# Token sums of the down projection: split where they are made, kept in DRAM in two parts, reloaded as operands

## The chip, the cores and the metric

The kernel runs on one core of one Trainium2 chip. The metric is the device time of one execution in microseconds (us). A core has a matrix engine (TensorE, PE in the profile, with PEld for its weight loads), a vector engine (VectorE, DVE), a scalar engine (ScalarE, ACT), a general engine (GpSimd, POOL) and a sync engine (SyncE, SP) whose queue here issues most of the transfers. Each engine works through its own instructions in order and waits at semaphores for the others. Transfers run on 16 DMA engines that all queues share.

## The reference, cut to what matters

The program is one decoder block on 256 tokens (plus 16 meta tokens) of width 2048: input projections, an RWKV-7 branch and a forgetting-attention branch, a gated merge, and a SwiGLU feed-forward part. The change concerns the last part:

```python
gate, up = jnp.split(_rms(h, n2) @ w_gu, 2, axis=-1)     # [256, 2048] @ [2048, 2 * 5632]
return h + (jax.nn.silu(gate) * up) @ w_dn               # [256, 5632] @ [5632, 2048]
```

Everything is float32. The kernel gets the precision on the matrix engine by splitting each operand in a high part (rounded to the engine's float32r) and a low part (the rest), and adding up high times high, low times high and high times low: three matrix instructions ("matmuls") for each product of blocks.

## The kernel before, in words

**Gate and up.** The hidden activations, transposed, split and normalised, lie in the tile `hts`: 16 slices (one per 128 rows of the contraction), each with a high and a low half of 272 columns, so 2176 bytes per partition and slice. For each of 11 blocks of 512 columns the kernel runs a gate job group and an up job group, each over 8 weight tiles of 512 KB (`raw`, four buffers, loaded by SP's queue). `wload` splits each into `wh` (ScalarE, line 335) and `wl` (VectorE, line 336), four buffers each. Jobs are written so that a tile is loaded and split one job ahead of its matmuls; a list scheduler then sets the final order on ScalarE, VectorE, GpSimd and SP in this part of the program, so that splits run up to three tiles ahead. After a group, `post_up` computes silu(gate) times up for four blocks of 128 columns (`ub`), and splits them into `ach` and `acl`, the operands of the down projection.

**Down.** The contraction of 5632 is cut into 22 pairs of 2 x 128 rows, the output of 2048 columns into two column halves (`cg` 0 and 1) of 1024. Pairs 10 to 21 (`SLOW`, "plain pairs") are done directly: two jobs of four products, so 8 products, 24 matmuls, in the PSUM tiles `dn`. Pairs 0 to 9 (`FAST`, "quads", since each has four jobs) use a Strassen-Winograd scheme: 7 products, 21 matmuls, with sums and differences of weight blocks (`tt`, made by VectorE on the way from the loaded tile `q`, lines 1516, 1523, 1524) and four sums of token blocks (`sx`, lines 1400 and 1401), of which three are operands of their own (`sst`) and the fourth overwrites a block of `ach` and `acl` that is not otherwise used for that pair. Four of the products go to PSUM tiles `dnp`, added at the end of a column half by `sums_of_products`. `ORDER` sets which pair follows which: 2 plain pairs first in column half 0, 1 in column half 1, and then quads and plain pairs in turn.

**The path of the token sums.** `sums_of_tokens` makes the four sums of a quad while the up group ends, and GpSimd's queue stores them in DRAM as float32 (`ss`, 256 KB each). The memory in which they are used later is still that of `hts`, so they cannot stay. Reloading is done two quads at a time by `sums_of` (line 1392) into one tile `sl`; a stream `split_of_sums`, woken about every 9 us of planned matmul time (`PAIRS`), splits it with ScalarE and VectorE (lines 510 and 511) into `sst` and into `ach` and `acl`, and then issues the next reload. The first reload is issued during gate and up; the second needs `sl` free, so it follows the first split, which needs the memory of `hts`, so the end of the last up group.

Of the kernel before, what the change touches and what calls it, by code (L numbers as in the profile page):

```python
# [9 lines left out]
F32 = mybir.dt.float32  # L10
F32R = mybir.dt.float32r
I32 = mybir.dt.int32
AF = mybir.ActivationFunctionType
ALU = mybir.AluOpType
# [4 lines left out]
P = 128  # L19
# [47 lines left out]

FAST = list(range(10))
SLOW = list(range(10, 22))
ORDER = [SLOW[:n] + [i for pair in zip(FAST, SLOW[n:]) for i in pair] + SLOW[n + len(FAST):] for n in (2, 1)]  # L70
PAIRS = 9000

HOP = 3050
SPREAD = 12000
# [2 lines left out]
GAP = 250  # L77
# [37 lines left out]
def hybrid_block(ctx, tc, A, out, dbg=None):  # L115
    nc = tc.nc
# [12 lines left out]
    dp = ctx.enter_context(tc.tile_pool(name="dp", bufs=1, space=DRAM))  # L129

    def main_ps(name):
        return psm.tile([P, 512], F32, tag="main", name=name)
# [176 lines left out]
        nc.tensor.matmul(pz, zw, zw, start=True, stop=True)  # L309


    behind = [None, None]

    def wload(parts, n, between=None, lay=None):

        raw = wp.tile([P, 1024], F32, tag="raw", name="raw", bufs=RAWB)
        wh = wp.tile([P, WCOLS], F32R, tag="wh", name="wh", bufs=WB)
        wl = wp.tile([P, WCOLS], F32R, tag="wl", name="wl", bufs=WB)  # L320
        if lay is not None:


            (_, _, shape, ((_, src),)), = parts
            odd, *first = lay
            nc.sync.dma_start(raw.rearrange("p (k c) -> p k c", c=shape[1]), src)
            if odd is None:
                rr = raw.rearrange("p (r c) -> p r c", c=T)
                th, tl = (t.rearrange("p (r c) -> p r c", c=L)[:, :, s:s + T] for t, s in zip((wh, wl), first))
            else:  # L330
                rr = raw.rearrange("p (j q c) -> p q j c", q=2, c=shape[1])
                th, tl = ((t if odd else t[:, s:s + 1024]).rearrange("p (q e) -> p q e", q=2)
                          [:, :, odd and s:(odd and s) + 512].rearrange("p q (j c) -> p q j c", c=shape[1])
                          for t, s in zip((wh, wl), first))
            behind[0] = nc.scalar.activation(th, rr, AF.Copy)  # L335
            behind[1] = nc.vector.tensor_tensor(tl, rr, th.bitcast(F32), op=ALU.subtract)  # L336
            return [(th, tl)]
        res = []
        for prow, c0, shape, srcs in parts:
            size = 1  # L340
            for d in shape:
                size *= d
            names = " ".join(f"d{i}" for i in range(len(shape)))
            kw = {f"d{i}": d for i, d in enumerate(shape)}

            def v(t):
                return t[:prow, c0:c0 + size].rearrange(f"p ({names}) -> p {names}", **kw)

            for sel, src in srcs:
                nc.sync.dma_start(v(raw)[sel], src)  # L350
            if between is not None:
                between(len(res))
            cs_ = slice(c0, c0 + size)
            nc.scalar.activation(wh[:prow, cs_], raw[:prow, cs_], AF.Copy)
            nc.vector.tensor_tensor(wl[:prow, cs_], raw[:prow, cs_], wh[:prow, cs_].bitcast(F32), op=ALU.subtract)
            res.append((v(wh), v(wl)))
        return res
# [3 lines left out]
    def kblock(ap):  # L361
        return ap.rearrange("(k p) c -> p k c", p=P)
# [13 lines left out]
    def spawn(gen, delay):  # L376
        streams.append([clock[0] + delay, gen, None])
# [44 lines left out]
    def finish_job():  # L422
        if pending:
            pending.pop()()

    def run(jobs):
        for load, mul in jobs:
            w = load()
            finish_job()
            pending.append(lambda w=w, mul=mul: mul(w))  # L430
# [78 lines left out]
    def split(hi, lo_, src):  # L509
        nc.scalar.activation(hi, src, AF.Copy)  # L510
        nc.vector.tensor_tensor(lo_, src, hi.bitcast(F32), op=ALU.subtract)  # L511
# [169 lines left out]
    def rwkv_jobs(g):  # L681
# [19 lines left out]
        def load():  # L701
            cs_ = slice(c0, c0 + 256)
            return wload([(96, 0, [2, 256], [((ALL, 0), A["rwkv_w2"][0][:, cs_]), ((ALL, 1), A["rwkv_a2"][0][:, cs_])]),
                          (P, 512, [2, 256], [((ALL,), kblock(A["rwkv_g2"][0][:, cs_]))])], 1024)
# [596 lines left out]
    hp = hp_pool.__enter__()  # L1301
    hh = hp.tile([P, 2, D], F32, tag="hh", name="hh")

    ht_pool = tc.tile_pool(name="ht", bufs=1, reuse_waits="tile")
    ht = ht_pool.__enter__()
    hts = ht.tile([P, KT, 2, L], F32R, tag="hts", name="hts")
    ss2 = hp.tile([P, 2, 4], F32, tag="ss2", name="ss2")
    rs2 = hp.tile([P, 2], F32, tag="rs2", name="rs2")
# [74 lines left out]
    NF = DFF // P  # L1383
# [2 lines left out]
    wgu = A["w_gate_up"][0]  # L1386
    ssd = {}

    def sums_of(at):
        sl = hp.tile([P, 2, 4, P], F32, tag="sl", name=f"sl{at}", bufs=1)  # L1390
        for x_ in range(2):
            nc.gpsimd.dma_start(sl[:, x_], ssd[FAST[at + x_]])
        return sl

    def sums_of_tokens(i, u0, u1):

        (a11, a21), (a12, a22) = ((u[:, :P], u[:, P:]) for u in (u0, u1))
        sx = ht.tile([P, 512], F32, tag="jk", name=f"sx{i}", bufs=2).rearrange("p (n c) -> p n c", n=4)
        for n, x_, y_, op in ((0, a21, a22, ALU.add), (1, sx[:, 0], a11, ALU.subtract), (2, a11, a21, ALU.subtract),
                              (3, a12, sx[:, 1], ALU.subtract)):  # L1400
            nc.vector.tensor_tensor(sx[:, n], x_, y_, op=op)
        d = ssd[i] = dp.tile([P, 4, P], F32, tag=f"ss{i}", name=f"ss{i}")
        nc.gpsimd.dma_start(d, sx)

    for j in range(DFF // 512):
        gs = [ht.tile([P, T], F32, tag="ga", name=f"ga{j}{m}", bufs=8) for m in range(4)]
# [26 lines left out]

    wdn = A["w_down"][0]
    fast = FAST
    sums0 = sums_of(0)
    slow = [i for i in range(NF // 2) if i not in fast]
    acp_h, acp_l = (t.rearrange("p (i k) (t c) -> p i k t c", k=2, t=2) for t in (ach, acl))
    finish_job()
    ht_pool.__exit__(None, None, None)  # L1440
    dn_pool = tc.tile_pool(name="dnp", bufs=1, reuse_waits="tile")
    dn = dn_pool.__enter__()
    sst = dn.tile([P, len(fast), 3, 2, P], F32R, tag="sst", name="sst")

    def split_of_sums(sl):

        for at in range(0, len(fast), 2):
            ps_ = slice(fast[at], fast[at] + 2)
            with tc.issue_after(behind[0].ins), tc.issue_after(behind[1].ins):
                split(sst[:, at:at + 2, :, 0, :], sst[:, at:at + 2, :, 1, :], sl[:, :, :3])  # L1450
                split(acp_h[:, ps_, 0, 1, :], acp_l[:, ps_, 0, 1, :], sl[:, :, 3])
            if at + 2 < len(fast):
                sl = sums_of(at + 2)
            yield PAIRS

    def a_of(i, k, t):
        return acp_h[:, i, k, t, :], acp_l[:, i, k, t, :]

    def s_of(i, n):
        return a_of(i, 0, 1) if n == 3 else tuple(sst[:, fast.index(i), n, a, :] for a in range(2))  # L1460

    def rows(ap):
        return ap.rearrange("p (r c) -> p r c", c=T)
# [13 lines left out]
    def slow_jobs(i, cg, cs, end):  # L1477
        def mk(x_):
            def load():
                j = 2 * cg + x_  # L1480
                return wload([(P, 0, [2, 512], [((ALL,), kblock(wdn[i * 256:(i + 1) * 256, j * 512:(j + 1) * 512]))])],
                             1024, lay=(None, *PLACE_T))

            def mul(w):
                if not cs:
                    cs.extend(main_ps(f"dn{cg}{n}") for n in range(4))
                first = i == slow[0]
                for t in range(2):
                    for k in range(2):
                        product(cs[2 * t + x_], a_of(i, k, t), w[0], k, first and k == 0, end and k == 1)  # L1490
                    if end:
                        post(cg, t, x_, cs[2 * t + x_])
            return load, mul
        return [mk(0), mk(1)]

    def fetch(i, cg):
        q = dn.tile([P, 2, 1024], F32, tag="q", name=f"q{cg}{i}", bufs=2)
        for k in range(2):
            nc.sync.dma_start(q[:, k, :], wdn[i * 256 + k * P:i * 256 + (k + 1) * P, cg * 1024:(cg + 1) * 1024])
        return q  # L1500

    def fast_jobs(i, cg, q, cs, ps, end):
# [27 lines left out]
        def load3():  # L1530
            return half_split(ts[1].rearrange("p x c -> p (x c)"))

        first = i == fast[0]

        def mul0(w):
            if not ps:
# [32 lines left out]
            nc.vector.tensor_tensor(hh[:, t, cs_], ps[:, c * n:(c + 1) * n], hh[:, t, cs_], op=ALU.add)  # L1569
            (nc.scalar if c else nc.sync).dma_start(out[0][t * P:(t + 1) * P, cs_], hh[:, t, cs_])  # L1570

    spawn(split_of_sums(sums0), GAP)
    quads = [(i, cg) for cg in range(2) for i in fast]
    got = {quads[0]: fetch(*quads[0])}
    for cg in range(2):
        cs, ps = [], []
        for i in ORDER[cg]:
            if i in fast:
                at = quads.index((i, cg)) + 1
                if at < len(quads):  # L1580
                    got[quads[at]] = fetch(*quads[at])
                run(fast_jobs(i, cg, got.pop((i, cg)), cs, ps, i == fast[-1]))
            else:
                run(slow_jobs(i, cg, cs, i == ORDER[cg][-1]))
    finish_job()
    dn_pool.__exit__(None, None, None)
    hp_pool.__exit__(None, None, None)
# [62 lines left out]
```

## Time and profile before

| | us |
|---|---|
| median of 3 runs | 1521.92 (1521.57 to 1523.06) |
| the profiled execution's own time | 1523.37 |
| its span, first to last instruction | 1521.7 |
| PE busy in the span | 1509.7 (99%) |
| VectorE, ScalarE, GpSimd busy | 1133.4, 817.7, 111.1 |
| mean granted TensorE clock | 0.997 of full speed |

The gate and up groups fill the span from about 795 to 1279 us, column half 0 of the down projection runs from 1279 to 1403, column half 1 from there to the end. In the profile a PE that is busy all the time says only that matmuls follow each other without a gap; how close they follow is read from their start times. Matmuls of 512 columns start 0.23 us apart when nothing holds them up, and the row of one says about 0.39 us because they overlap. "PE dnp" and "PE dn" are the matmuls of the down projection, "gt" and "up" those of gate and up. Idle time of an engine counts only where the chain that ends last passes through it.

### The profile page before, as it was taken

The page shows a single profiled execution, that of the slowest core. Times are in us where ns is not written, and L with a number is a line of the kernel's source. Part 1 is how long each engine was busy: PE and PEld are TensorE (multiplying, and loading weights), DVE is VectorE, ACT ScalarE, POOL GpSimd, SP SyncE. Part 2 cuts the span into 40 slices and gives each one's busy share as a digit, 9 for nine tenths or more (in the row PEclk, how much of TensorE's full clock was granted, in tenths as well). Part 3 has the DMA queues.
Part 4 walks back from the last instruction along what each step waited for, and adds up shares of the span by engine and source line. Part 5 has one row for each costly group of instructions (what it writes and reads, how often), then busy time and mean ns, then how long its engine had stood idle before and what let it go on. Part 6 is the DMA issues. An engine that isn't in the chain of part 4 may idle for free.

```text
span 1521.7 us, 26190 instructions
## 1 busy us (share of the span) xinstructions
PE 1509.7 (99%) x10053; PEld 1337.7 (88%) x10053; DVE 1133.4 (74%) x2019; ACT 817.7 (54%) x1236; POOL 111.1 (7%) x202
## 2 busy tenths in 40 slices
PE   9999999999999999999999999999999999899999
PEld 9999999999989888998888888888888888688887
DVE  8888699689689757876565666666556656989987
ACT  7664565475465545554455455455445544655553
POOL 2112202202202000000000000000000000000000
PEclk9999999999999999999999999999999999999999
DMA  8567456646645757786666766666666666666762
GB/s 272 165 167 211 117 157 186 170 122 173 188 133 151 221 146 220 225 268 208 181 180 192 213 204 199 207 197 200 188 188 192 182 194 219 208 215 195 232 213 85
DMA packets 208414, 288.57 MB, mean 190 GB/s; under 512 B 24416, under 2 KB 129392, under 8 KB 208288
## 3 DMA queue, kind: packets, MB, share of 16 engines
q1 hardware_dynamic: 201792, 277.25, 61.6%
q0 software_dynamic: 1600, 5.24, 0.9%
q10 hardware_dynamic: 4896, 4.40, 0.9%
q8 instruction: 79, 1.29, 0.3%
q14 instruction: 47, 0.39, 0.1%
HBM read 276.98 MB, written 9.87 MB: 189 GB/s over the span
## 4 chain that ended last, share of the span: by engine, by line
PE 96%; DVE 2%; DMA 1%; ACT 1%; issue 0%; SPq 0%; POOL 0%; DVEq 0%; ACTq 0%
PE gt L441 11%; PE up L441 11%; PE zg L441 8%; PE gt L443 5%; PE up L443 5%; PE zg L443 4%; PE dn L1468 4%; PE dn L1469 4%; PE dn L1470 4%; PE f L441 2%; PE br L365 2%; PE br L366 2%; PE br L367 2%; PE f L365 2%; PE wo L1331 2%; PE wo L1333 2%
## 5 line engine op out<-in xcount | busy, mean ns | idle before, releaser
L336 DVE TENSOR_TENSOR wl<-raw,wh 128x1024 fp32r<-128x1024 f32 x448 | 547.5, 1227 | 273.6 <-ACT wh L335 273.0
L335 ACT ACTIVATE wh<-raw 128x1024 fp32r<-128x1024 f32 x448 | 472.9, 1058 | 444.2 <-PE up L441 119.9
L441 PE MATMUL gt<-hts,wh 128*128 128x512 f32 x704 | 243.4, 393 | 0.0
L441 PE MATMUL up<-hts,wh 128*128 128x512 f32 x704 | 243.1, 393 | 0.0
L443 PE MATMUL gt<-hts,wl 128*128 128x256 f32 x660 | 185.1, 280 | 0.0
L443 PE MATMUL up<-hts,wl 128*128 128x256 f32 x660 | 184.9, 280 | 0.0
L441 PE MATMUL zg<-xhl,wh 128*128 128x512 f32 x512 | 181.2, 400 | 0.0
L441 PEld LDWEIGHTS up<-hts,wh 128*128 128x128 f32 x704 | 130.0, 188 | 25.1
L441 PEld LDWEIGHTS gt<-hts,wh 128*128 128x128 f32 x704 | 130.0, 188 | 25.0
L443 PE MATMUL zg<-xhl,wl 128*128 128x256 f32 x480 | 134.5, 280 | 0.0
L443 PEld LDWEIGHTS up<-hts,wl 128*128 128x128 f32 x660 | 125.5, 190 | 1.9
L443 PEld LDWEIGHTS gt<-hts,wl 128*128 128x128 f32 x660 | 125.5, 190 | 1.9
L441 PEld LDWEIGHTS zg<-xhl,wh 128*128 128x128 f32 x512 | 94.3, 188 | 18.6 <-issue 0.7
L1468 PE MATMUL dn<-wh,ach 128*128 128x512 f32 x252 | 100.3, 398 | 0.7 <-ACT wh L510 0.7
L1469 PE MATMUL dn<-wh,acl 128*128 128x512 f32 x252 | 99.6, 395 | 0.0
L1470 PE MATMUL dn<-wl,ach 128*128 128x512 f32 x252 | 98.8, 395 | 0.1
L443 PEld LDWEIGHTS zg<-xhl,wl 128*128 128x128 f32 x480 | 91.1, 190 | 1.2
L510 ACT ACTIVATE wh<-tt 128x1024 fp32r<-128x1024 f32 x40 | 42.5, 1062 | 71.3 <-PE dn L1469 57.3
L365 PE MATMUL f<-xhl,wh 128*128 128x272 f32 x256 | 76.0, 297 | 0.0
L367 PE MATMUL f<-xhl,wl 128*128 128x272 f32 x256 | 73.7, 288 | 0.0
L366 PE MATMUL f<-xhl,wh 128*128 128x272 f32 x256 | 73.7, 288 | 0.0
L511 DVE TENSOR_TENSOR wl<-tt,wh 128x1024 fp32r<-128x1024 f32 x40 | 49.0, 1225 | 19.9 <-ACT wh L510 19.4
(496 smaller groups left out, 3171.8 us busy)
## 6 DMA issues: line engine op xcount, KB each, us to landing
raw<-in_w_gate_up_dram SPq DMA_DIRECT2D x176, 512.0 KB, 4.2
raw<-in_w_in_dram SPq DMA_DIRECT2D x160, 512.0 KB, 4.0
raw<-in_w_down_dram SPq DMA_DIRECT2D x48, 512.0 KB, 4.5
q<-in_w_down_dram SPq DMA_DIRECT2D x40, 512.0 KB, 5.9
raw<-in_w_o_dram SPq DMA_DIRECT2D x32, 512.0 KB, 4.5
raw<-in_w_branch_a_dram SPq DMA_DIRECT2D x16, 512.0 KB, 4.7
raw<-in_w_branch_b_dram SPq DMA_DIRECT2D x16, 512.0 KB, 4.5
zgd<-zg ACTq DMA_DIRECT2D x30, 128.0 KB, 3.8
```

What stands on the lines that cost most here:

```text
L335: behind[0] = nc.scalar.activation(th, rr, AF.Copy)
L336: behind[1] = nc.vector.tensor_tensor(tl, rr, th.bitcast(F32), op=ALU.subtract)
L365: nc.tensor.matmul(ps, wh, ah, start=first, stop=False)
L366: nc.tensor.matmul(ps, wh, al, start=False, stop=False)
L367: nc.tensor.matmul(ps, wl, ah, start=False, stop=last)
L441: nc.tensor.matmul(ps.rearrange("p (a t) -> p a t", a=2), wh, act, start=first, stop=last)
L443: nc.tensor.matmul(ps[:, :T], wl, act[:, 0, :], start=False, stop=False)
L510: nc.scalar.activation(hi, src, AF.Copy)
L511: nc.vector.tensor_tensor(lo_, src, hi.bitcast(F32), op=ALU.subtract)
L1468: nc.tensor.matmul(o, a[0], hi, start=first, stop=False)
L1469: nc.tensor.matmul(o, a[1], hi, start=False, stop=False)
L1470: nc.tensor.matmul(o, a[0], lo_, start=False, stop=last)
```

## The change

1. The sums of a quad are split into a high and a low part at once, in the up group (`sr`, one buffer, by ScalarE and VectorE), and both parts are stored in DRAM (512 KB a quad).
2. The stream `split_of_sums`, the tile `sl` and its wake-up `PAIRS` are gone. In their place `sums_of(i)` has GpSimd's queue load the three sums of quad i, both parts, straight into `sst` (384 KB), and the fourth into `ach` and `acl` (64 KB each). The tile in DRAM is float32 and the one on the chip float32r, so these are converting transfers. All loads for quads 0 to 8 are written before the first job of the down projection.
3. Column half 0 starts with four plain pairs instead of two. There are only twelve plain pairs, so quad 9 is done as a plain pair in column half 0, at its end (`QUICK`). Its fourth sum may overwrite `ach` and `acl` only after that, so `finish_job` is called at the end of column half 0, and then `sums_of(9)`.
4. In the memory of gate and up an unused tile `shift` of 128 bytes a partition stands before `hts`. As `sl` is gone too, `hts` moves from byte 80896 to byte 76928 of a partition; `sst` and what follows it in the down projection move down by 4096 bytes.

```diff
-ORDER = [SLOW[:n] + [i for pair in zip(FAST, SLOW[n:]) for i in pair] + SLOW[n + len(FAST):] for n in (2, 1)]
-PAIRS = 9000
+ORDER = [SLOW[:4] + [i for pair in zip(FAST, SLOW[4:] + FAST[-1:]) for i in pair],
+         SLOW[:1] + [i for pair in zip(FAST, SLOW[1:]) for i in pair] + SLOW[11:]]
+QUICK = [FAST[:-1], FAST]
...
     ht = ht_pool.__enter__()
+    ht.tile([P, 32], F32, tag="shift", name="shift")
     hts = ht.tile([P, KT, 2, L], F32R, tag="hts", name="hts")
...
-    def sums_of(at):
-        sl = hp.tile([P, 2, 4, P], F32, tag="sl", name=f"sl{at}", bufs=1)
-        for x_ in range(2):
-            nc.gpsimd.dma_start(sl[:, x_], ssd[FAST[at + x_]])
-        return sl
...
-        d = ssd[i] = dp.tile([P, 4, P], F32, tag=f"ss{i}", name=f"ss{i}")
-        nc.gpsimd.dma_start(d, sx)
+        sr = ht.tile([P, 2, 4, P], F32R, tag="sr", name=f"sr{i}", bufs=1)
+        split(sr[:, 0], sr[:, 1], sx)
+        d = ssd[i] = dp.tile([P, 2, 4, P], F32, tag=f"ss{i}", name=f"ss{i}")
+        nc.gpsimd.dma_start(d, sr.bitcast(F32))
...
-    sst = dn.tile([P, len(fast), 3, 2, P], F32R, tag="sst", name="sst")
-
-    def split_of_sums(sl):
-
-        for at in range(0, len(fast), 2):
-            ps_ = slice(fast[at], fast[at] + 2)
-            with tc.issue_after(behind[0].ins), tc.issue_after(behind[1].ins):
-                split(sst[:, at:at + 2, :, 0, :], sst[:, at:at + 2, :, 1, :], sl[:, :, :3])
-                split(acp_h[:, ps_, 0, 1, :], acp_l[:, ps_, 0, 1, :], sl[:, :, 3])
-            if at + 2 < len(fast):
-                sl = sums_of(at + 2)
-            yield PAIRS
+    sst = dn.tile([P, len(fast), 2, 3, P], F32R, tag="sst", name="sst")
+
+    def sums_of(i):
+        nc.gpsimd.dma_start(sst[:, fast.index(i)], ssd[i][:, :, :3])
+        for a, t in enumerate((acp_h, acp_l)):
+            nc.gpsimd.dma_start(t[:, i, 0, 1, :], ssd[i][:, a, 3])
...
-    spawn(split_of_sums(sums0), GAP)
-    quads = [(i, cg) for cg in range(2) for i in fast]
+    quads = [(i, cg) for cg in range(2) for i in QUICK[cg]]
     got = {quads[0]: fetch(*quads[0])}
+    for i in QUICK[0]:
+        sums_of(i)
...
+        if cg == 0:
+            finish_job()
+            for i in QUICK[1]:
+                if i not in QUICK[0]:
+                    sums_of(i)
```

**The order on ScalarE, at the first quad of column half 0, before** (q00 is the weight tile of quad 0, `sl2` the reloaded sums of quads 2 and 3):

```order
L510 ACTIVATE sst_14448<-sl0_14397 128x6x128
L510 ACTIVATE wh_14526<-q00_14449 128x2x256
L510 ACTIVATE wh_14551<-q00_14449 128x4x256
L510 ACTIVATE sst_14448<-sl2_14475 128x6x128
L510 ACTIVATE ach_9877<-sl2_14475 128x2x128
L510 ACTIVATE wh_14565<-tt_14530 128x4x256
L510 ACTIVATE wh_14575<-tt_14555 128x4x256
```

and now:

```order
L335 ACTIVATE wh_14608<-raw_14607 128x4x256
L335 ACTIVATE wh_14626<-raw_14625 128x4x256
L510 ACTIVATE wh_14646<-q00_14477 128x2x256
L510 ACTIVATE wh_14664<-q00_14477 128x4x256
L510 ACTIVATE wh_14678<-tt_14650 128x4x256
L510 ACTIVATE wh_14688<-tt_14668 128x4x256
```

The split of the second reload stood between the quad's second and third weight split; now nothing stands there, and the weight splits of the fourth plain pair come ahead.

**The order on SP's queue at the same place**, as one piece of the difference (`-` before, `+` now):

```order
-L326 DMA raw<-in_w_down_dram 128x2x512 x8
-L1499 DMA q_14449<-in_w_down_dram 128x1024 x2
-L1499 DMA q_14523<-in_w_down_dram 128x1024 x2
-L1499 DMA q_14615<-in_w_down_dram 128x1024 x2
+L326 DMA raw<-in_w_down_dram 128x2x512 x10
+L1488 DMA q_14477<-in_w_down_dram 128x1024 x2
+L1488 DMA q_14643<-in_w_down_dram 128x1024 x2
```

Ten loads of plain weight tiles now stand ahead of the first quad's weights, where eight stood.

**The order on VectorE between the column halves, before** (dn00 to dn03 are the PSUM tiles of column half 0; the last two `wl` are the two weight tiles of the first plain pair of column half 1):

```order
L1569 TENSOR_TENSOR hh_9122<-dn02_14466,hh_9122 128x512
L336 TENSOR_TENSOR wl_15378<-raw_15376,wh_15377 128x4x256
L1569 TENSOR_TENSOR hh_9122<-dn01_14465,hh_9122 128x512
L1569 TENSOR_TENSOR hh_9122<-dn03_14467,hh_9122 128x512
L336 TENSOR_TENSOR wl_15400<-raw_15398,wh_15399 128x4x256
```

and now:

```order
L1558 TENSOR_TENSOR hh_9122<-dn02_14521,hh_9122 128x512
L1558 TENSOR_TENSOR hh_9122<-dn01_14520,hh_9122 128x512
L1558 TENSOR_TENSOR hh_9122<-dn03_14522,hh_9122 128x512
L336 TENSOR_TENSOR wl_15411<-raw_15409,wh_15410 128x4x256
L336 TENSOR_TENSOR wl_15417<-raw_15415,wh_15416 128x4x256
```

The first weight split of column half 1 moved behind the two last sums of column half 0. On PE ten matmuls that need only `wh` now stand ahead of the first that needs this `wl`, where six stood.

More of the change, by code (lines that the diff above doesn't have):

```diff
@@ L309, in hybrid_block @@
         nc.tensor.matmul(pz, zw, zw, start=True, stop=True)
-    behind = [None, None]
     def wload(parts, n, between=None, lay=None):
@@ L334, in wload @@
                           for t, s in zip((wh, wl), first))
-            behind[0] = nc.scalar.activation(th, rr, AF.Copy)
-            behind[1] = nc.vector.tensor_tensor(tl, rr, th.bitcast(F32), op=ALU.subtract)
+            nc.scalar.activation(th, rr, AF.Copy)
+            nc.vector.tensor_tensor(tl, rr, th.bitcast(F32), op=ALU.subtract)
             return [(th, tl)]
@@ L1435, in hybrid_block @@
     fast = FAST
-    sums0 = sums_of(0)
-    slow = [i for i in range(NF // 2) if i not in fast]
     acp_h, acp_l = (t.rearrange("p (i k) (t c) -> p i k t c", k=2, t=2) for t in (ach, acl))
@@ L1459, in s_of @@
     def s_of(i, n):
-        return a_of(i, 0, 1) if n == 3 else tuple(sst[:, fast.index(i), n, a, :] for a in range(2))
+        return a_of(i, 0, 1) if n == 3 else tuple(sst[:, fast.index(i), a, n, :] for a in range(2))
     def rows(ap):
@@ L1486, in mul @@
                     cs.extend(main_ps(f"dn{cg}{n}") for n in range(4))
-                first = i == slow[0]
+                first = i == ORDER[cg][0]
                 for t in range(2):
@@ L1531, in load3 @@
             return half_split(ts[1].rearrange("p x c -> p (x c)"))
-        first = i == fast[0]
+        first = i == QUICK[cg][0]
         def mul0(w):
@@ L1577, in hybrid_block @@
         for i in ORDER[cg]:
-            if i in fast:
+            if i in QUICK[cg]:
                 at = quads.index((i, cg)) + 1
@@ L1581, in hybrid_block @@
                     got[quads[at]] = fetch(*quads[at])
-                run(fast_jobs(i, cg, got.pop((i, cg)), cs, ps, i == fast[-1]))
+                run(fast_jobs(i, cg, got.pop((i, cg)), cs, ps, i == QUICK[cg][-1]))
             else:
                 run(slow_jobs(i, cg, cs, i == ORDER[cg][-1]))
+        if cg == 0:
[3 more added lines that the diff above has]
+                    sums_of(i)
     finish_job()
```

## The prediction

> **What bounds the kernel now.** I first read busy time in stretches: gate and up, the first 30 us of the down projection, the rest of column half 0, and four microseconds on their own. The columns are the stretch, its length, then PE, PEld, DVE, ACT and POOL in us busy (instructions), granted clock, DMA share, GB/s:
>
> ```profile
> 795.00:1276.00 481.00, 481.00 (x2771) 423.99 (x2770) 302.82 (x476) 240.62 (x343) 6.74 (x12) 1.00 0.67 196
> 1276.00:1306.00 30.00, 25.18 (x98) 18.87 (x97) 22.89 (x36) 14.99 (x23) 2.58 (x5) 0.89 0.64 218
> 1306.00:1405.00 99.00, 99.00 (x430) 80.42 (x429) 89.43 (x97) 56.46 (x61) 1.77 (x4) 1.00 0.66 212
> ...
> 1298.00:1302.00 4.00, 3.14 (x7) 2.04 (x8) 3.95 (x5) 3.08 (x4) 0.14 (x1) 0.55 0.74 244
> ```
>
> PE fills every stretch except the one at 1276 to 1306, where it idles 4.8 us and its clock falls. So time can be won at that place, by fewer matmuls, or by denser ones. Next PE's waits at that place (us in all, count, longest):
>
> ```profile
> PE dnp L1468 <- ACT wh L510: 3.4, 2, 2.8
> PE dn L1468 <- ACT wh L510: 0.7, 1, 0.7
> PE dnp L1470 <- DVE wl L511: 0.6, 1, 0.6
> ```
>
> They add up to 4.7 us, and all are weight splits of the first quad. The chain of waits says why those are late (start, length, engine), and ScalarE's own timeline confirms it:
>
> ```profile
> 1285.87 0.97 DVE sst L511
> 1287.13 0.54 POOL sl L1392
> 1287.67 6.56 DMA sl<-ss
> 1294.32 0.85 ACT sst L510
> ```
>
> ```profile
> 1288.14 0.63 ACT L510 ACTIVATE wh<-q 128x512 fp32r<-128x512 f32 x1 [2.30 <-DMA q<-in_w_down_dram]
> 1290.55 1.06 ACT L510 ACTIVATE wh<-q 128x1024 fp32r<-128x1024 f32 x1 [1.78 <-DMA q<-in_w_down_dram]
> ...
> 1295.37 1.04 ACT L510 ACTIVATE wh<-tt 128x1024 fp32r<-128x1024 f32 x1
> ```
>
> ScalarE, having split `q`, stands before the split of the second reload, which lands at 1287.67 + 6.56 = 1294.2; the quad's next weight split (1295.37) is queued behind it, and PE behind that. The weights themselves were there at 1290.5. What the episode costs is read from matmul starts: the first one of the down projection, the first of quad 0, the first of quad 1, and the same pair of marks at a later quad of the half:
>
> ```profile
> 1279.04 0.39 PE L1468 MATMUL dn<-wh,ach 128*128 128x512 f32 x1
> ...
> 1290.08 0.39 PE L1468 MATMUL dnp<-wh,ach 128*128 128x512 f32 x1
> ...
> 1309.43 0.39 PE L1468 MATMUL dnp<-wh,ach 128*128 128x512 f32 x1
> ...
> 1382.09 0.39 PE L1468 MATMUL dnp<-wh,ach 128*128 128x512 f32 x1
> ...
> 1392.46 0.39 PE L1468 MATMUL dnp<-wh,ach 128*128 128x512 f32 x1
> ```
>
> A quad and the plain pair behind it are 21 + 24 = 45 matmuls. Undisturbed they take 1392.46 - 1382.09 = 10.37 us, 0.230 each; at quad 0 they take 1309.43 - 1290.08 = 19.35. **The episode costs 8.98 us**: 4.7 of waits, and about 4.3 of slow matmuls (clock 0.55) and restarts.
>
> The Trainium skill (TensorE: Matmul & The Clock Gate, Part 1: The HAM clock gate) has the clock halve only after an idle window of some 3.4 us; the longest wait in the rows has 2.8 us and the clock still fell, so the trace disagrees. By that rule the episode would cost its 4.7 us of waits alone, and the sum below would come to 1518.2; the starts of the matmuls decide against it.
>
> **The change part by part.** *Splits and the second reload leave column half 0.* Nothing of the sums is left in ScalarE's order between the quad's weight splits, and nothing waits for `sl`. The loads wait only for the end of the last up matmul, at about 1279, and the first operand made of them is needed in the quad's second and third job. The two added plain pairs put 48 matmuls ahead; the 48 of the first two took 1290.08 - 1279.04 = 11.04 us, so quad 0 starts at 1279.04 + 2 x 11.04 = 1301.1. Are sums and weights there by then? Page and transfer rows (queue: packets, MB, share of 16 engines; then issues, size, median us to landing), and SP's timeline for the quad's weights:
>
> ```profile
> q0 software_dynamic: 1600, 5.24, 0.9%
> ...
> sl<-ss POOLq DMA_DIRECT2D x10, 256.0 KB, 4.3
> ss<-sx POOLq DMA_DIRECT2D x10, 256.0 KB, 4.7
> ```
>
> ```profile
> 1282.48 17.23 SPq L1499 DMA_DIRECT2D q<-in_w_down_dram  x6
> ```
>
> Sums: 512 KB a quad, twice what one reload of 256 KB carries in 4.3 us (6.56 at the longest). Even at 2 x 6.56 from 1279.04 quad 0 has its sums at 1292.2, 9 us early, and one quad follows per 10.37 us. Nine quads are 4.7 MB; the queue's 5.24 MB of before took 0.9% of 1521.7 = 13.7 us of all engines, so these take 12.3, and the DMA share of 0.66 leaves a third free: 36 us to drain them all, during which weights have 45 us of quads. So at plain speed they are hidden.
>
> Weights of quad 0: `q` was issued at 1282.48 behind eight plain tiles, and its halves started the split at 1288.14 and the subtraction at 1290.49, 5.7 and 8.0 us later. Now ten tiles stand ahead, and the tenth has to wait until the sixth is split. The buffer of that split comes free after two jobs, 24 matmuls, at 1279.04 + 5.5 = 1284.6, and the split takes 1.06 on ScalarE and 1.23 on VectorE: `q` is issued at about 1287.5 and lands at 1293.2 and 1295.5. Behind it VectorE does four steps in the order shown:
>
> ```profile
> 1290.49 1.23 DVE L1516 TENSOR_TENSOR tt<-q 128x1024 f32<-128x1024 f32 x1 [1.00 <-DMA q<-in_w_down_dram]
> ...
> 1402.37 0.69 DVE L1569 TENSOR_TENSOR hh<-dn,hh 128x512 f32<-128x512 f32 x1
> 1402.97 1.22 DVE L336 TENSOR_TENSOR wl<-raw,wh 128x1024 fp32r<-128x1024 f32 x1
> ```
>
> 1.23 + 0.69 + 0.69 + 1.22 = 3.8, so the `wl` of its second job is there at 1299.3; PE asks for it after five matmuls, at 1301.1 + 1.15 = 1302.2. Three microseconds of slack: the stall goes, **-8.98**. Bounds: all of it, or none of it.
>
> *One product more.* Column half 0 has 9 quads and 13 plain pairs instead of 10 and 12: 24 - 21 = 3 matmuls, 3 x 0.23 = **+0.69**.
>
> *The boundary between the halves.* VectorE now does the two last sums of half 0 ahead of the first weight split of half 1. Before, PE began half 1 thus, with six matmuls ahead of the first that needs `wl`:
>
> ```profile
> 1402.82 0.39 PE L1468 MATMUL dn<-wh,ach 128*128 128x512 f32 x1
> ...
> 1404.25 0.50 PE L1470 MATMUL dn<-wl,ach 128*128 128x512 f32 x1
> ```
>
> Shifted to that clock, the two sums (0.60 apart, since 1402.97 - 1402.37 = 0.60) run at 1402.97 and 1403.57, the split at 1404.17 to 1405.39. Ten matmuls that need no `wl` cover 1402.82 + 10 x 0.23 = 1405.12. **+0.3**; bounds 0 and, if only six matmuls cover it, 1405.39 - 1404.20 = +1.2.
>
> *Splits in gate and up.* Ten quads, each a split of 128x512: by the rows above 0.63 on ScalarE and 0.69 on VectorE, 13 us in all, and a store of 512 KB instead of 256. VectorE is busy 302.82 of 481 us there and ScalarE 240.62, and weight splits run up to three tiles ahead (12 matmuls each, 8.3 us). The one buffer `sr` may hold VectorE up until the last store has landed, 4.7 us for half the size, which that lead covers too: **0**. Without the lead, up to 10 x 0.69 = 7 us would show.
>
> *128 bytes on.* The slices of `hts` are 2176 = 17 x 128 bytes apart, so neighbours lie differently within 256 bytes, and the up matmuls alternate, these two and so on in turn:
>
> ```profile
> 1224.81 0.40 PE L441 MATMUL up<-hts,wh 128*128 128x512 f32 x1
> ...
> 1225.16 0.39 PE L441 MATMUL up<-hts,wh 128*128 128x512 f32 x1
> ```
>
> Moving all by 128 swaps the long with the short: **0**. Were the cause something that the move changes for all, 0.01 us for half of the 1408 gate and up matmuls is 7 us, either way.
>
> **The sum**, against the profiled execution: 1523.37 - 8.98 + 0.69 + 0.3 = 1515.4. Its own time is 1.45 above the median of the runs, 1521.92; taken off, **1513.9 us**.
>
> **The rivals.** *A part of the stall stays (0.18).* The quad's weights and up to nine quads of sums travel together. If they share evenly and `q` takes twice as long (11.4 and 16 us from 1287.5) it lands at 1303.5, its `wl` is ready at 1307.3, and PE waits 1307.3 - 1302.2 = 5.1 us: 1519.0. A smaller delay gives 1515 to 1518. For it: the longest reload took 6.56 us against a median of 4.3 while VectorE was busy 22.89 of 30 us. Against: three microseconds of slack, and a DMA share of 0.64 in that stretch. The Trainium skill (SBUF — State Buffer, SBUF: two separate sides) warns that descriptors which GpSimd writes for its transfers starve while VectorE holds the shared port in its two-port modes; VectorE's subtractions from two SBUF sources take less of it by the same section. That the 6.56 us come from this no row here shows; if they did, this rival would be the likelier.
>
> *The converting transfers are slow (0.08); the case on the other side.* No row shows a transfer that converts. If its packets take c times as long, the 12.3 us of engine time become 12.3c. With both queues backlogged the weights get half the engines where they need 0.66, so for 24.6c us they fall behind by 24%, 5.9c us. Four loaded tiles of 12 matmuls (2.76 us each) cover 11 us. PE waits from c = 1.9 on, and the gain of 8.0 us is used up at 5.9c = 19, c = 3.2. With c = 4 the wait is 23.6 - 11 = 12.6 us, and the time 1526.5. Against: the nearest rows, the plain reloads, spread by 6.56 / 4.3 = 1.5 at most, under the 1.9 at which waiting begins; I take 1.
>
> *The full stall only moves (0.05).* Some other wait of 5 us at quad 0 or 1 drops the clock again: 1522.9, no change. For it: quad 1's first subtraction stands in VectorE's order ahead of quad 0's last `wl`, and its `q` arrives one transfer later, with about 1 us to spare.
>
> *The move by 128 bytes acts on all (0.06).* Half of the time to the good, 1507; half to the bad, 1521, no change.
>
> **How the numbers follow.** The forecast case has 0.63. Its own range is 1512 to 1516. The range for 8 in 10 reaches up into the partial stall, 1518.9, and down into a part of a gain by the move, 1510.6. About 0.2%, 3 us, can be told from no change here. Faster: 0.63 + 0.18 + 0.03, less 0.01 for partial stalls that reach 1519, 0.83. Same: full stall 0.05 + bad move 0.03, 0.08. Slower: 0.08 of slow transfers, and 0.01 of partial stalls with the clock's fall on top, 0.09.
>
> **What would show it.** Right: from the first matmul of quad 0 to that of quad 1 it takes 10.4 us; no fall of the granted clock after 1279; the first matmul of quad 0 about 22 us after the first of the down projection; gate and up as long as before (PE full from 795 to 1276); ScalarE's weight splits of quad 0 back to back. A partial stall would stand as a wait of PE on `wl` of the first quad with `q` as what VectorE waited for. Slow transfers would show as queue 0's share of the engines far above 2% (twice 0.9%), as `raw` landing late and PE waiting on L335 during the plain pairs. An act of the move would show in the mean of the gt and up matmuls and in a longer or shorter stretch before 1276. Wrong I am if quad 0's weights come later than 1302 on that clock, or if gate and up change by over a microsecond.

## The result, and the profile after

The changed kernel takes 1515.74 us (1515.47 to 1515.90, six runs), the kernel before, run beside it, 1522.14 (1520.75 to 1523.10): a ratio of 0.9958, interval 0.9945 to 0.9971. It is 6.4 us faster; 8.0 were forecast, and 1515.74 lies inside the range of 1510.6 to 1518.9. Three far slower executions, two of 2465 us and one of 2988, are left out of all ratios and traces below.

The stretches of the changed kernel, with the columns of the prediction's first fence:

```profile
795.00:1276.00 481.00, 481.00 (x2776) 424.20 (x2776) 309.26 (x484) 247.06 (x353) 15.25 (x28) 1.00 0.68 203
1276.00:1306.00 30.00, 29.07 (x129) 23.24 (x128) 21.13 (x31) 14.87 (x21) 7.04 (x10) 1.00 1.03 333
1306.00:1405.00 99.00, 98.87 (x429) 80.18 (x428) 89.16 (x96) 53.52 (x56) 1.07 (x2) 1.00 0.66 214
```

The clock no longer falls, and PE idles 0.93 us in the second stretch instead of 4.8. But the DMA share of that stretch has gone from 0.64 to 1.03: by the profile's count all DMA engines are taken. PE's waits that are left there, and PE's marks (first gate matmul, first of the down projection, first of quad 0, first of quad 1, the boundary of the halves with the gap behind it, the last matmul):

```profile
PE dnp L1459 <- DVE wl L511: 0.5, 1, 0.5
PE dn L1459 <- DVE wl L511: 0.4, 1, 0.4
```
```profile
788.48 0.39 PE L441 MATMUL gt<-hts,wh 128*128 128x512 f32 x1
...
1278.03 0.40 PE L1457 MATMUL dn<-wh,ach 128*128 128x512 f32 x1
...
1300.11 0.39 PE L1457 MATMUL dnp<-wh,ach 128*128 128x512 f32 x1
...
1311.95 0.39 PE L1457 MATMUL dnp<-wh,ach 128*128 128x512 f32 x1
...
1394.88 0.39 PE L1457 MATMUL dn<-wh,ach 128*128 128x512 f32 x1
...
1396.98 0.40 PE L1458 MATMUL dn<-wh,acl 128*128 128x512 f32 x1
1397.51 0.50 PE L1459 MATMUL dn<-wl,ach 128*128 128x512 f32 x1
...
1509.87 0.39 PE L1459 MATMUL dn<-wl,ach 128*128 128x512 f32 x1
```

The first gate matmul and the last matmul of the kernel before:

```profile
788.63 0.40 PE L441 MATMUL gt<-hts,wh 128*128 128x512 f32 x1
...
1517.53 0.39 PE L1470 MATMUL dn<-wl,ach 128*128 128x512 f32 x1
```

Put side by side, these marks say where every microsecond went:

| stretch, us | before | after | change | forecast |
|---|---|---|---|---|
| up to the first gate matmul | 788.63 | 788.48 | -0.15 | 0 |
| gate and up | 490.41 | 489.55 | -0.86 | 0 |
| plain pairs ahead of quad 0 | 11.04 | 22.08 | +11.04 | +11.04 |
| quad 0 and the pair behind it | 19.35 | 11.84 | -7.51 | -8.98 |
| rest of column half 0 | 93.39 | 82.93 | -10.46 | -11.04 + 0.69 |
| column half 1 to the last matmul | 114.71 | 114.99 | +0.28 | +0.3 |

They add up to -7.66; the profiled executions' own times differ by 1523.37 - 1515.74 = 7.63. Quad 0 and its pair take 1.47 us more than 10.37, because its weights came late. ScalarE's splits of them, VectorE's first subtraction, and SP's issue:

```profile
1296.34 0.63 ACT L510 ACTIVATE wh<-q 128x512 fp32r<-128x512 f32 x1 [6.17 <-DMA q<-in_w_down_dram]
1298.07 1.06 ACT L510 ACTIVATE wh<-q 128x1024 fp32r<-128x1024 f32 x1 [1.11 <-DMA q<-in_w_down_dram]
```
```profile
1297.99 1.23 DVE L1505 TENSOR_TENSOR tt<-q 128x1024 f32<-128x1024 f32 x1 [0.30 <-DMA q<-in_w_down_dram]
```
```profile
1286.71 2.20 SPq L1488 DMA_DIRECT2D q<-in_w_down_dram  x4
```

Issue was at 1286.71, as foreseen (1287.5), but the halves landed 9.6 and 11.3 us later, not 5.7 and 8.0. What ran beside them: GpSimd's queue issued seven loads of sums in 4.92 us, and the last of the ten at 1288.95. Quad 9's three sums are among the ten, since only its fourth sum has to wait for the end of the column half.

```profile
1278.76 4.92 POOL L1441 DMA_DIRECT2D sst<-ss  x7 [252.20 <-PE up L441]
...
1288.95 0.71 POOL L1441 DMA_DIRECT2D sst<-ss  x1 [1.45 <-DMA sst<-ss]
```

From that landing on VectorE works without a gap, with quad 1's first subtraction in its order ahead of quad 0's last `wl`, which is done at 1305.34; so the second wait, 0.49 us, comes from the same lateness as the first.

### The profile page after: what moved, and what is told of

It is laid out like the page before. It is cut to its first block, busy times and chain, and to the rows that moved or that the text cites. A ratio compares the mean times of both kernels' runs of the same rounds, so it can differ in the third digit from the quotient of the medians.

```text
span 1514.0 us, 26216 instructions
## 1 busy us (share of the span) xinstructions
PE 1505.9 (99%) x10056; PEld 1335.8 (88%) x10056; DVE 1130.9 (75%) x2014; ACT 817.8 (54%) x1234; POOL 123.5 (8%) x222
## 4 chain that ended last, share of the span: by engine, by line
PE 97%; DVE 2%; DMA 0%; issue 0%; ACT 0%; SPq 0%; DVEq 0%
PE gt L441 11%; PE up L441 11%; PE zg L441 8%; PE gt L443 5%; PE up L443 5%; PE dn L1459 4%; PE dn L1457 4%; PE dn L1458 4%; PE zg L443 4%; PE f L441 2%; PE br L365 2%; PE br L366 2%; PE br L367 2%; PE f L365 2%; PE wo L1332 2%; PE wo L1334 2%
```

## The experiments

All were timed against the kernel before on the same chip; comparisons with the changed kernel go across such sets, in which the medians of the kernel before lie between 1521.7 and 1522.4. "Quad 0 and its pair" is the time from the first matmul of quad 0 to that of quad 1, 10.37 us undisturbed; "gate and up" runs from the first gate matmul to the first of the down projection.

### The 128 bytes

The changed kernel without the tile:

```diff
-    ht.tile([P, 32], F32, tag="shift", name="shift")
```

> The changed kernel without the 128-byte tile ahead of the hidden activations (they lie 128 bytes lower). The trace of the changed kernel shows gate and up shorter by 0.9 us (489.5 for 490.4). Theory: that is the move; without it the stretch takes 490.4 again and the time is 1516.6. Rival, as forecast: the move only swaps long and short matmuls, and the 0.9 us are scatter between executions; 1515.7 and 489.5 to 490.4 without a pattern.

1516.47 us (1516.29 to 1516.70), 0.73 above the changed kernel, and the two sets of runs don't overlap. Gate and up took 490.4:

```profile
788.17 0.40 PE L441 MATMUL gt<-hts,wh 128*128 128x512 f32 x1
...
1278.60 0.39 PE L1456 MATMUL dn<-wh,ach 128*128 128x512 f32 x1
```

The kernel before with that line added was the counter-test:

> The kernel before, with the 128-byte tile alone. Theory (the move makes matmuls denser): gate and up take 489.5 instead of 490.4, time 0.9 below the kernel before, about 1521.2; the stall at the first quad stays at about 9 us. Rival (the move does nothing): 1522.1. The two lie within the scatter of the kernel before, so the stretch in the trace decides.

1521.69 us, ratio 0.9996 (0.9987 to 1.0005): the times can't tell, as foreseen. The stretch is read from the trace of a further single run:

> The kernel before with the 128-byte tile alone, for its trace. Theory: gate and up (first gate matmul to first of the down projection) take 489.6 us as in every trace so far of a kernel with the tile, against 490.4 in every one without it. Rival: 490.4, the gain needs something else of the change.

1522.68 us; gate and up take 489.6, and quad 0 and its pair still 19.39:

```profile
788.16 0.39 PE L441 MATMUL gt<-hts,wh 128*128 128x512 f32 x1
...
1277.74 0.40 PE L1469 MATMUL dn<-wh,ach 128*128 128x512 f32 x1
```

Over the thirteen traces of this study read so, the eight with the tile (the changed kernel's among them) have 489.5 to 489.6 and the five without it 490.4, whatever else differs. The move is worth 0.86 us on its own. Gate and up have 1408 matmuls of 512 columns and as many of 256, so this is 0.3 ns a matmul. The other tiles of that memory move by 128 bytes too, but of what moves only `hts` is an operand of these matmuls. How its address acts on them was not tried.

### What crowds the first quad's weights

```diff
     def sums_of(i):
-        nc.gpsimd.dma_start(sst[:, fast.index(i)], ssd[i][:, :, :3])
+        if i < 3:
+            nc.gpsimd.dma_start(sst[:, fast.index(i)], ssd[i][:, :, :3])
...
-        return a_of(i, 0, 1) if n == 3 else tuple(sst[:, fast.index(i), a, n, :] for a in range(2))
+        return a_of(i, 0, 1) if n == 3 else tuple(sst[:, fast.index(i) % 3, a, n, :] for a in range(2))
```

> The changed kernel with the three sums of quads 0 to 2 alone loaded, and used for all quads (so the output is another); it leaves out seven of the ten 384 KB loads. In the changed kernel the first quad's weights land at 1296.3 and 1298.0, 9.6 and 11.3 us after their issue, and quad 0 with its plain pair takes 11.84 instead of 10.37 us. Theory: the ten loads share the DMA engines with these weights; with three of them the weights land by 1294, the quad takes 10.4, time 1514.3. Rival: the weights are late because SP issues them behind ten plain tiles (1286.7); they land late here too, quad 0 stays at 11.8 and the time at 1515.7.

1513.97 us (1513.94 to 1514.59). Quad 0 and its pair take 10.37 us without a wait, and with the issue at 1286.43 the weights land 2 us earlier:

```profile
1294.19 0.63 ACT L510 ACTIVATE wh<-q 128x512 fp32r<-128x512 f32 x1 [4.36 <-DMA q<-in_w_down_dram]
1295.72 1.06 ACT L510 ACTIVATE wh<-q 128x1024 fp32r<-128x1024 f32 x1 [0.90 <-DMA q<-in_w_down_dram]
```

The other seven loads, which quad 0 doesn't need, made its weights late enough to be waited for. With three loads beside them they land 7.8 and 9.3 us after their issue, still later than the 5.7 and 8.0 of the kernel before.

### Each half of the change alone

The new path with the old order:

```diff
-ORDER = [SLOW[:4] + [i for pair in zip(FAST, SLOW[4:] + FAST[-1:]) for i in pair],
-         SLOW[:1] + [i for pair in zip(FAST, SLOW[1:]) for i in pair] + SLOW[11:]]
-QUICK = [FAST[:-1], FAST]
+ORDER = [SLOW[:n] + [i for pair in zip(FAST, SLOW[n:]) for i in pair] + SLOW[n + len(FAST):] for n in (2, 1)]
+QUICK = [FAST, FAST]
```

> The new path of the sums with the old order (two plain pairs first, ten quads in column half 0, so three matmuls fewer). Theory: the new path alone doesn't remove the stall, since quad 0 starts at 1289 and its weights, sharing the DMA engines with ten loads of sums, are split only at about 1297; a wait of some 7 us, with a fall of the clock, 1519 to 1525. Rival: the split of the second reload in ScalarE's order was the whole of it; then at most 2 us of waiting are left and the time is 1514 to 1516.

1519.60 us, ratio 0.9986 (0.9977 to 0.9995): by the ratio 2.1 us gained, of which 0.86 are the 128 bytes. PE:

```profile
1291.06 0.51 PE L1456 MATMUL dnp<-wh,ach 128*128 128x512 f32 x1 [1.96 <-ACT wh L509]
...
1293.50 0.79 PE L1456 MATMUL dn<-wh,ach 128*128 128x512 f32 x1 [1.23 <-ACT wh L509]
...
1305.92 0.39 PE L1456 MATMUL dnp<-wh,ach 128*128 128x512 f32 x1
```

Quad 0 starts 2.1 us late (1291.06 for 1288.93) and then takes 14.86, so 6.6 us are lost where 9.0 were (7.5 to 9.6 in three traces of the kernel before, see below); the clock in 1292 to 1296 is 0.55. The split in ScalarE's order was not the whole of the stall: with it gone, weights that come too late for this start take its place.

The old path with the lead:

```diff
-ORDER = [SLOW[:n] + [i for pair in zip(FAST, SLOW[n:]) for i in pair] + SLOW[n + len(FAST):] for n in (2, 1)]
+ORDER = [SLOW[:4] + [i for pair in zip(FAST, SLOW[4:11]) for i in pair] + FAST[7:] + SLOW[11:],
+         SLOW[:1] + [i for pair in zip(FAST, SLOW[1:]) for i in pair] + SLOW[11:]]
```

> The kernel before (float32 sums, one reload tile, splits during the down projection), with four plain pairs first in column half 0 and all ten quads kept (the last three without a plain pair between). Theory: the lead of two more plain pairs is what pays, on whichever path: the second reload is split during the plain pairs or at quad 0 with time to spare, the stall falls from 9 to at most 2 us, time 1513.5 to 1515.5. Rival: in ScalarE's order the third reload's split now stands between quad 0's weight splits and is as late as the second was; the stall moves, 1519 to 1523.

1523.76 us, ratio 1.0013 (1.0004 to 1.0022): nothing gained. Quad 0 and its pair take 17.15, 2.2 less than in the kernel before. ScalarE and the chain:

```profile
1295.21 0.63 ACT L511 ACTIVATE wh<-q 128x512 fp32r<-128x512 f32 x1 [4.52 <-PE dn L1470]
1301.56 0.84 ACT L511 ACTIVATE sst<-sl 128x768 fp32r<-128x768 f32 x1 [5.72 <-DMA sl<-ss]
...
1302.62 1.04 ACT L511 ACTIVATE wh<-q 128x1024 fp32r<-128x1024 f32 x1
```
```profile
1290.35 0.55 POOL sl L1393
1290.90 10.58 DMA sl<-ss
1301.56 0.85 ACT sst L511
```

The second reload is issued 3.2 us later (1290.35, not 1287.13), and it takes 10.58 us instead of 6.56, beside the weights of two quads and two plain tiles, which SP's queue issues from 1287.90 to 1292.55 (that these slow it down is argued, not tried). Its split still stands among quad 0's, so most of the lead is eaten up; it is the second reload, and not the third as the rival had it, that does this. PE's wait for it is a single one of 2.16 us, and the clock fell right behind it (columns as in the stretches above):

```profile
1303.71 0.79 PE L1469 MATMUL dn<-wh,ach 128*128 128x512 f32 x1 [2.16 <-ACT wh L511]
```
```profile
1304.00:1308.00 4.00, 3.41 (x8) 2.21 (x8) 3.97 (x5) 0.74 (x2) 1.09 (x2) 0.50 0.56 165
```

The 2.2 us gained at quad 0 are lost again later: from the first matmul of quad 1 to the last matmul this order takes 200.3 us, and the kernel before, less two plain pairs, 208.1 - 11.0 = 197.1. What is lost lies around the end of column half 0 (1380 to 1420), where three quads follow each other without a plain pair between; PE waits 0.8, 0.6 and 0.4 us on weight splits there.

```profile
1317.85 0.39 PE L1469 MATMUL dnp<-wh,ach 128*128 128x512 f32 x1
...
1518.17 0.39 PE L1471 MATMUL dn<-wl,ach 128*128 128x512 f32 x1
```

So in time the path alone brings 1.2 us and the move 0.86, the lead alone nothing, all together 6.4. At the first quad, where the order at the end of the half plays no part, the path alone saves 2.4 us of the first trace's 9.0, the lead alone 2.2, and both 7.5. These are single traces, and in the kernel before this stretch varies by 2.05 us; but against each of its three traces both together save more than the two alone added.

### Conversion, and when the loads come

The same loads without conversion, on the same queue:

```diff
-    sst = dn.tile([P, len(fast), 2, 3, P], F32R, tag="sst", name="sst")
+    sst = dn.tile([P, len(fast), 2, 3, P], F32, tag="sst", name="sst")
...
-            nc.gpsimd.dma_start(t[:, i, 0, 1, :], ssd[i][:, a, 3])
+            nc.gpsimd.dma_start(t[:, i, 0, 1, :].bitcast(F32), ssd[i][:, a, 3])
...
-        return a_of(i, 0, 1) if n == 3 else tuple(sst[:, fast.index(i), a, n, :] for a in range(2))
+        return a_of(i, 0, 1) if n == 3 else tuple(sst[:, fast.index(i), a, n, :].bitcast(F32R) for a in range(2))
```

> The changed kernel with the sums loaded without conversion (the tile on the chip is float32 too and read as float32r by the matmuls), on the same queue. Theory: it is the bytes that crowd out the first quad's weights (in the 44 us from 1276 the sums take 13.5 us of all engines for 3.93 MB, 3.4 us per MB, the weights 2.9), so little changes: 1515.3 to 1515.8. Rival: the conversion makes the loads slow, and plain ones free the engines early enough: 1514.3.

1518.94 us (1518.41 to 1521.10): 3.2 slower than the changed kernel, which neither theory had. Queues in 1280 to 1300 (packets, MB, share of 16 engines), the changed kernel and then the plain loads; q1 carries the weights, q0 the sums:

```profile
q1 hardware_dynamic: 1519, 3.87, 54.8%
q0 software_dynamic: 2107, 3.06, 53.3%
```
```profile
q0 software_dynamic: 1120, 3.93, 55.4%
q1 hardware_dynamic: 1360, 3.38, 43.5%
```

The engines are full in both. A converting packet carries 3.06 MB / 2107 = 1.5 KB and costs 0.533 x 20 / 3.06 = 3.5 us of all engines per MB; a plain one 3.5 KB and 2.8. So conversion does slow a load, by 1.24 in this company (the weights' own cost goes from 2.8 to 2.6 us per MB, so a part of it may be the neighbour's), but the plain sums move faster at the weights' expense, which get 3.38 MB instead of 3.87. Median landings go from 14.7 to 9.4 us for the sums, and from 9.5 to 13.4 for quads' weights. The quad's second half is split only at 1301.25, PE waits 0.63, 0.43 and 2.07 us within 5.1 us, and the clock falls, as two microseconds soon after show (columns as in the stretches above):

```profile
1307.00:1309.00 2.00, 2.00 (x6) 1.58 (x5) 2.00 (x3) 0.66 (x2) 0.00 (x0) 0.50 0.91 342
```

The Trainium skill (DMA: Bandwidth & Descriptors, Queues, rings and completion order) says that an engine takes turns between its queues by whole packets; larger packets on one queue then mean more bytes for it, and these bytes agree in direction. In size they don't: as long as both queues have work, equal turns would give them equally many packets, and the weights and the sums moved 1519 and 2107 of the profile's packets, then 1360 and 1120. The order of packets within an engine is not shown by any run here.

The plain type lets SP's queue carry the loads too, one quad at a time (`behind[0]` is the last load of a plain weight tile):

```diff
     def sums_of(i):
-        nc.gpsimd.dma_start(sst[:, fast.index(i)], ssd[i][:, :, :3])
+        with tc.issue_after(behind[0].ins):
+            nc.sync.dma_start(sst[:, fast.index(i)], ssd[i][:, :, :3])
...
                 run(slow_jobs(i, cg, cs, i == ORDER[cg][-1]))
+                if late and i >= SLOW[2]:
+                    sums_of(late.pop(0))
```

> Plain loads of the sums again, but on SP's queue, one quad's behind the weight loads of each plain pair from the third on, so that they come one by one and the first quad's weights stand ahead of them. Theory: with nothing to share with, the first quad's weights land within 8 us of their issue; quad 0 and its pair take 10.4 us instead of 11.8, time 1514.3. Rival: the loads in SP's queue hold up the weights behind them, or a quad's sums come too late; a wait of a microsecond or more at each quad, 1517 to 1525.

1514.03 us (1513.74 to 1514.10), ratio to the kernel before 0.9950 (0.9937 to 0.9962), 1.7 below the changed kernel. The table of PE's waits has none left in the down projection (the gap at the boundary is still there). The weights of quad 0, issued at 1286.49, land 6.3 and 8.7 us later, and quad 0 and its pair take 10.37:

```profile
1292.82 0.63 ACT L512 ACTIVATE wh<-q 128x512 fp32r<-128x512 f32 x1 [3.01 <-DMA q<-in_w_down_dram]
...
1295.29 1.06 ACT L512 ACTIVATE wh<-q 128x1024 fp32r<-128x1024 f32 x1 [1.84 <-DMA q<-in_w_down_dram]
```

```profile
1299.81 0.39 PE L1460 MATMUL dnp<-wh,ach 128*128 128x512 f32 x1
...
1310.18 0.39 PE L1460 MATMUL dnp<-wh,ach 128*128 128x512 f32 x1
```

The run differs from the changed kernel in the type of the loads, in their queue and in their time. The plain type alone made the kernel slower, so what gains here is when, and on which queue, the loads come.

With a shorter lead on top: `ORDER` starts column half 0 with three plain pairs, keeps all ten quads, and puts the first quad's weights ahead of the fourth pair's.

> As the spread loads, with three plain pairs first and all ten quads in column half 0 (three matmuls fewer), and the first quad's weights queued ahead of the fourth plain pair's. Theory: quad 0 starts at about 1294.6 and its weights, issued at 1278 to 1280, are split by then; no stall, 0.7 below the spread loads: 1513.6. Rival: 16.6 us are too short a lead for weights and sums together, a stall of 2 us or more remains: 1515.5 or above.

1514.82 us (1514.38 to 1515.65), no gain. There is no stall at quad 0 (10.40), but the matmuls saved are lost elsewhere. Two quads follow each other without a pair between at the end of half 0, PE waits 0.4 us at the boundary and 0.5 behind it, and column half 1 takes 116.3 us instead of 115.0; the order with three quads in a row, above, lost time at the same place. And a wait of 0.8 us stands far ahead of gate and up, on a weight split of the first part of the program that the edit does not touch; it comes to 789.1 at the first gate matmul. Whether that one belongs to the kernel or to the execution is open.

Last, the boundary: as the spread loads, with the early end of half 0 taken out and quad 9's sums loaded after the first plain pair of half 1.

```diff
-        if cg == 0:
-            finish_job()
-            for i in QUICK[1]:
-                if i not in QUICK[0]:
-                    sums_of(i)
+                if cg == 1 and i == ORDER[1][0]:
+                    sums_of(FAST[9])
```

> The spread loads (1514.03) with the sums of quad 9 loaded after the first plain pair of column half 1 instead of behind an early end of column half 0, which puts VectorE's order between the halves back: the first weight split of half 1 stands ahead of the last two sums of half 0 again. Theory: the gap of 0.3 us on PE at that place goes, column half 1 takes 114.7 instead of 115.0 us, time 1513.7. Rival: the gap is hidden or moves to the next wait, 1514.0.

1513.83 us (1513.48 to 1514.82), ratio 0.9945 (0.9932 to 0.9959). The first `wl` matmul of half 1 follows the one ahead of it by 0.26 us, as in the kernel before, where it was 0.53 in the changed kernel, and column half 1 takes 114.71 us up to the last matmul:

```profile
1393.97 0.40 PE L1461 MATMUL dnp<-wh,acl 128*128 128x512 f32 x1
1394.23 0.50 PE L1462 MATMUL dn<-wl,ach 128*128 128x512 f32 x1
```

By the marks the gap is gone; the 0.2 us between the medians lie within the scatter of the runs.

### Where the kernel before scatters

> The kernel before again, unchanged, for a second trace of it. Its times scatter over 4 to 5 us, those of the changed kernel over 0.5. Theory: the scatter sits in the stall at the first quad (19.35 us there in the first trace, whose execution took 1523.37); this execution's time differs from that by as much as its quad 0 and pair differ from 19.35, within 0.5 us. Then the 1.45 us that the forecast took off as an offset of the execution belong to the stall, and went with it. Rival: the scatter lies elsewhere, and this stretch is 19.3 again whatever the time.

> A third trace of the kernel before, for the same question and with the same expectations as the second.

They took 1523.14 and 1521.46 us. The first matmuls of quad 0 and of quad 1 in the first, then in the second:

```profile
1289.24 0.39 PE L1468 MATMUL dnp<-wh,ach 128*128 128x512 f32 x1
...
1309.20 0.39 PE L1468 MATMUL dnp<-wh,ach 128*128 128x512 f32 x1
```
```profile
1289.61 0.39 PE L1468 MATMUL dnp<-wh,ach 128*128 128x512 f32 x1
...
1307.52 0.39 PE L1468 MATMUL dnp<-wh,ach 128*128 128x512 f32 x1
```

Quad 0 and its pair took 19.96 and 17.91 us, against 19.35 in the first trace. The theory is missed in its bound: the first differs by +0.61 there and by -0.23 in all, the second by -1.44 and -1.91. The rest, -0.85 and -0.47, is there before the down projection starts (1278.19 and 1278.57, for 1279.04). So two places scatter, the stall by 2.05 us and the part ahead of gate and up by 0.85 in three executions, and the two account for both differences.

## Why the prediction was right, and where it was not

- **What bounds the kernel** was read rightly: the whole of the gain but the move's lies at the first quad of column half 0, and the experiments with half of the change show that the late reload's split in ScalarE's order had to go for the lead to count, and that its going alone saves only about 2 us there.
- **The stall: -8.98 forecast, -7.51 measured.** The step that failed is the landing of quad 0's weights. Their issue and the four steps of VectorE behind it came as worked out (1.2 + 0.7 + 0.7 + 1.2 us), but the transfer was priced with rows of the kernel before, 5.7 and 8.0 us, and it took 9.6 and 11.3: with three loads of sums beside it 7.8 and 9.3, with the loads one by one behind it 6.3 and 8.7. The slack of 3 us was used up, and 0.44 and 0.49 us of waits with what follows each make the 1.47. So the mechanism that came is that of the first rival, the partial stall, to which 0.18 was given, and the time lies in the 1515 to 1518 that it named for a smaller delay. Its price of 5.1 us was too high because it let the transfer take twice as long, 16 us. The working counted the sums' 12.3 us of engine time as drained through the third that the weights leave free; but all ten loads were issued within 11 us, and in 1280 to 1300 the sums took 53.3% of the engines where the weights had 54.8%. They were 3.93 MB, not 4.7, since nine of the fourth sums had been loaded during gate and up.
- **The signs that were named** say the same: no fall of the clock and quad 0 22.1 us behind the first matmul of the down projection, as in the forecast case, but 11.84 us instead of 10.4 for quad 0 and its pair, splits of its weights that are not back to back, and a wait of PE on a `wl` of quad 0 with `q` as what VectorE waited for.
- **The move by 128 bytes: 0 forecast, -0.86 measured.** Long and short matmuls did change places, but the trade isn't even. The bounds of 7 us either way held it; the value chosen did not.
- **One product more, +0.69; splits in gate and up, 0; the boundary, +0.3.** The rest of column half 0 changed by -10.46, 0.1 from -11.04 + 0.69. The working there took 12 matmuls to a weight tile of gate and up; there are 16, in the same 2.8 us, so the lead of three tiles is 8.3 us either way. In gate and up VectorE did 6.4 us and ScalarE 6.4 us more in the profiled stretch, and PE lost nothing by it: without the move the stretch is as long as before. The boundary cost 0.28, and went when VectorE's order was put back.
- **Slow converting transfers** are real, 1.24 times a plain one with all engines busy, under the 1.9 at which the rival had waiting begin. What the rival missed is that a slower load is the gentler neighbour.
- **The clock.** A fall needed less than the 3.4 us of the Trainium skill's rule (TensorE: Matmul & The Clock Gate, Part 1: The HAM clock gate): in the old path with the lead a single wait of 2.16 us was enough for a fall to 0.50, and with the new path in the old order waits of 1.96 and 1.23 us within 4.4 us gave 0.55; with waits of 0.44 and 0.49 us in the changed kernel it stayed at 1.00.
- **The offset of 1.45 us** between profiled execution and median was taken off the sum. Against its own execution the sum was 1515.4, and the profile after has 1515.74: that it came so near is luck, as the two misses of 1.47 and 0.86 have opposite signs. Taking the offset off assumed that it stays when the stall goes; but the changed kernel's profiled execution lies on its median, the stall is one of the two places that scatter in the kernel before, and the changed kernel's runs spread by 0.4 us where those of before spread by 2.4. The 1.8 us between 1513.9 and 1515.74 are 1.47 - 0.86 + 1.45, less 0.15 us ahead of gate and up and 0.1 in the rest of column half 0.

## What to carry to other kernels

When transfers are made independent of everything, ask what they will share the engines with: count the bytes that can be in flight at once, not only the engine time that is free on average, and queue what is needed first ahead of what is needed later. Of a stall with two causes in line, mending one gave about 2 us here and mending both 7.5, so try each part alone before pricing it. And when the place that is mended is also where the runs scatter, work the forecast out on the profiled execution's own scale and don't subtract its distance from the median.

## What the runs showed of the hardware

- Moving the operand `hts` by 128 bytes changes the time of gate and up's 2816 matmuls by 0.86 us in all, in eight traces against five without an exception.
- With all engines busy, converting loads of sums left the weights 3.87 MB in 20 us and plain ones 3.38, so the faster transfer made the kernel slower by 3.2 us.
- TensorE's clock fell to half after a single wait of 2.16 us; two waits of 0.44 and 0.49 us left it at 1.00.
